# Copying a residual state to HBM in eight queued pieces instead of two

## The chip, the cores and the metric

The kernel runs on one core of one Trainium2 chip. The metric is the device time of one execution in microseconds (us), and the number that is compared is the median of several executions. A profiled execution gives the trace: for each engine every instruction with its start, its duration and what it waited for.

## What is computed

One decoder layer, on x of 256 tokens by 2048 columns, all in float32. The part of the reference that matters here:

```python
h = rms_norm(x, mix_norm_g[i]);  z = h @ w_in[i]          # mixers A (mLSTM) and B (attention) from z
x = x + jnp.concatenate([ha, hb], axis=-1) @ w_out[i]     # 2048 x 2048
h = rms_norm(x, ffn_norm_g[i])
u = h @ w_up[i]                                           # 2048 x 11264
a, g = jnp.split(u, 2, axis=-1);  a = causal_dwconv(a, conv_w[i], conv_b[i])
x = x + (jax.nn.gelu(a, approximate=False) * g) @ w_down[i]
gate = jax.nn.sigmoid(rms_norm(x, ple_norm_g[i]) @ w_ple_gate[i])
x = x + gate * (p[i].astype(x.dtype) @ w_ple_proj[i])
```

The x after w_out is the residual state of this document. It is used twice: at once, normalised, as the left operand of w_up; and much later, when the product with w_down is added to it.

## The kernel before, in words

**Products.** Every float32 operand of a product is held as two parts, a rounded one (`hi`) and the rest (`lo`), and a product is three matmuls (`three`, lines 361 to 364): hi by hi, hi by lo, lo by hi. A weight block arrives by DMA in a raw buffer; `part` (line 294, and line 1291 in the feed-forward stage) casts it to `hi` on ScalarE (line 295 or 1292) and subtracts on VectorE for `lo` (line 297 or 1294). So each block of weights costs a DMA of 512 KB, one cast, one subtraction and 12 matmuls of 512 columns.

**Plain blocks and seven-blocks.** In w_out, w_up and others some pairs of weight rows are multiplied with seven products in place of eight. Such a pair is a group of four blocks, written "a" four times or "b" four times in an order string: the first loads two raw buffers and multiplies one product, each of the others multiplies two. The splits of the third and the fourth add halves of the two raw buffers with VectorE (lines 435, 436, 446 and 447), so the group holds both raw buffers until its fourth split. "p" is a plain block. `OUT_ORDERS` (line 54) holds one order of 20 blocks for each half of the output columns of w_out; the second is that of the output columns 1024 to 2047.

**Streams.** `run_stream` (line 267) writes the program for the blocks up to and with w_out. At block i it splits blocks up to i + 3 and loads as many further blocks as there are free raw buffers: three named `raw` and, in this part, four more (`morex`). Then it writes the block's matmuls, and after them whatever hook was put on the block with `with_after`. `run_units` (line 1300) does the same for the feed-forward blocks, with splits up to four blocks ahead; its raw buffers are the three `raw`, four more (`u32r`, `u36r`) from block 7 on, and `v4`, the half of row tile 0 of `xs` with the columns 1024 to 2047, from block 26 on. The loads, the copies of this change and some layout moves (`move`, line 202, 32 KB each, which go out on SyncE and GpSimd) are DMAs that SyncE issues, one after the other in one queue. A DMA whose operands are not ready holds up all that stand behind it on SyncE.

**The order on an engine is not that of the source.** The program is handed to a scheduler that orders each engine's instructions by an estimate of time, keeping to the dependencies. `tc.issue_after(ins)` adds the one constraint that what the block issues on the engine of `ins` stands behind `ins`. `traced()` returns the last instruction written. `between` (line 1685) puts its hook behind the last cast, the last subtraction and the last load.

**The residual state.** It lives in SBUF in `xs`, 128 partitions by 2 row tiles by 2048 columns. `evac`, `combined` and line 1035 add the w_out products to it. The feed-forward stage needs the space: row tile 1 becomes `z_up` (line 1123, written by lines 1761 to 1764 at the end of the seven-blocks of each w_up group), and row tile 0 becomes `c_` (line 1139) and the raw buffer `v4`. So the state is copied to a DRAM tile `kept_x` (line 79) by `keep_x` and comes back by `move_x` (line 1125) late in the w_down stage. `keep_x(0)`, the columns 0 to 1023, is hooked on block 8 of the second w_out order; `keep_x(1)`, the columns 1024 to 2047, on block 8 of the first w_up group, whose order is "pppppp" "apapapap" "bpbbbp".

Of the kernel before, what the change touches and what calls it, by code (L numbers as in the profile page):

```python
# [50 lines left out]
TURN_AT = (-1, -1, 0, 0)  # L51
GATE_ORDER = "ppppp" "apapapap" "bpbpbb" "p"
OUT_K = (8, 9, 10, 11, 12, 13, 14, 15, 0, 1, 2, 3, 4, 5, 6, 7)
OUT_ORDERS = ("pppp" "apapapap" "bpbpbpb" "p", "pp" "apapapa" "bpbpbb" "ppppp")
ACT_AT = (9, 10, 11, 12, 13, 14, 15, 16, 17, 18)


# [1 line left out]
def layer_kernel(  # L59
# [6 lines left out]
    nc = tc.nc  # L66
# [12 lines left out]
    kept_x = kp.tile([P, NT, D], F32, name="kept_x")  # L79

    def keep_x(i):
        c = slice(i * 1024, (i + 1) * 1024)
        nc.sync.dma_start(out=kept_x[:, :, c], in_=xs[:, :, c])

    def bank(tag, name):
        return ps.tile([P, 512], F32, tag=tag, name=name)
# [1 line left out]
    def f32(ap):  # L88
        return ap.bitcast(F32)
# [8 lines left out]
    xs = bp.tile([P, NT, D], F32, name="xs")  # L98
# [84 lines left out]
    def rstd_of(ssq, name):  # L183
        tot = sm.tile([P, NT], F32, name=f"tot_{name}")
        dve.tensor_reduce(out=tot, in_=ssq, axis=AX.X, op=ALU.add)
        r = sm.tile([P, NT], F32, name=f"rstd_{name}")
        rsqrt_mean(r, tot, D)
        return r
# [40 lines left out]
    last = {}  # L229

    def traced():

        return nc.cur_bb.bb.instructions[-1]
# [7 lines left out]
    def pull(n):  # L241

        while n > 0 and side:
            turn[0] ^= 1
            job = side[min(turn[0], len(side) - 1)]
            try:
                next(job)
                n -= 1
            except StopIteration:
                side.remove(job)  # L250

    def pull_all():
        rush.append(1)
        pull(10 ** 6)
        rush.clear()
# [11 lines left out]
    def run_stream(blocks, pulls, more, ramp=False):  # L267

        nb = len(blocks)
        held, used = set(), {}  # L270
        raw_tags = [f"raw{i}" for i in range(RAW)]

        def free(j):
            tags = [t for t in [*raw_tags, *more] if t not in held and (t in raw_tags or more[t][0] <= j < more[t][1])]
            return sorted(tags, key=lambda t: used.get(t, -1))

        def put(j):
            b = blocks[j]
            if b.load is not None:
                b.load()  # L280
            b.raws, b.tags = [], free(j)[: len(b.srcs)]
            for t, src in zip(b.tags, b.srcs):
                held.add(t)
                kb, n = src.shape[1], src.shape[2]
                raw = wp.tile([P, BLK], F32, tag=t, name=f"raw{j}", bufs=1) if t in raw_tags else more[t][2]()
                nc.sync.dma_start(out=raw[:, : kb * n].rearrange("p (k n) -> p k n", k=kb), in_=src)
                b.raws.append(raw)

        def give(tags):
            for t in tags:  # L290
                held.remove(t)
                used[t] = max(used.values(), default=0) + 1

        def part(hi, lo, raw):
            act.copy(hi, raw)  # L295
            last["hi"] = traced()
            dve.tensor_sub(lo, raw, f32(hi))  # L297

        loaded = split = 0
        for i in range(-RAW, nb):  # L300
            ahead = min(AHEAD_SPLIT, 1 + i // 2) if ramp else AHEAD_SPLIT
            while True:
                if loaded < nb and (i >= -1 or loaded <= i + RAW) and len(free(loaded)) >= len(blocks[loaded].srcs):
                    put(loaded)
                    loaded += 1
                elif i >= -1 and split < min(nb, i + ahead + 1, loaded):
                    j, split = split, split + 1
                    b = blocks[j]
                    if b.prep is not None:
                        b.prep()  # L310
                    hi = wp.tile([P, BLK], F32R, tag=f"hi{j % PARTS}", name=f"hi{j}", bufs=1)
                    lo = wp.tile([P, BLK], F32R, tag=f"lo{j % PARTS}", name=f"lo{j}", bufs=1)
                    if b.own is not None:
                        give(b.own(part, hi, lo))
                        b.parts = hi, lo
                        continue
                    kb, n = b.srcs[0].shape[1:3]
                    hi, lo = hi[:, : kb * n], lo[:, : kb * n]
                    part(hi, lo, b.raws[0][:, : kb * n])
                    give(b.tags)  # L320
                    b.parts = [v.rearrange("p (k n) -> p k n", k=kb) for v in (hi, lo)]
                else:
                    break
            if i >= 0:
                blocks[i].fn(*blocks[i].parts)
                done[0] += 1
                pull(pulls)
# [174 lines left out]
    with mixers:  # L502
# [430 lines left out]
        def with_after(b, hook):  # L933
            fn = b.fn
            b.fn = lambda hi, lo: (fn(hi, lo), hook())
# [86 lines left out]
        def out_group(g_):  # L1022

            st = {}

            def places(h):
                if h == 0:
                    return squares("x2y"), mp.tile([P, NT * 4, 128], F32, tag="col", name="x2z")
                v = [mk_place[:, i * BLK : (i + 1) * BLK] for i in range(2)]
                return v[0].rearrange("p (t b c) -> p t b c", t=NT, b=4), v[1].rearrange("p (a c) -> p a c", c=P)  # L1030

            def evac(t, h, o):
                c = 2 * g_ + h
                xc = xs[:, t, c * 512 : (c + 1) * 512]
                dve.tensor_add(xc, o, xc)
                if g_:
                    return
                if t == 0:
                    st[h] = places(h)
                square(st[h][0], t, 0, xc)  # L1040
                if t == NT - 1:
                    move(*st[h], nc.sync if h else None)
                    side.append(columns((st[h][1], done[0]), get_x2T, c * 4, g_ffn))

            def added():
                for h in range(2):
                    sumsq(ssq2, 2 * g_ + h, 512)

            def combined(p1, p5, p6, p7):
                c0 = g_ * 1024  # L1050
                x00, x01, x10, x11 = (xs[:, t, c0 + n * 512 : c0 + (n + 1) * 512] for t in range(NT) for n in range(2))
                right = xs[:, :, c0 + 512 : c0 + 1024]
                a = mqT.rearrange("p g a c -> p (g a c)")[:, g_ * 512 : (g_ + 1) * 512]
                act.copy(a, p1)
                dve.tensor_add(x00, p1, x00)
                dve.tensor_add(a, p6, a)
                dve.tensor_add(right, p5.unsqueeze(1).broadcast_to([P, 2, 512]), right)
                dve.tensor_sub(x01, x01, a)
                dve.tensor_add(a, p7, a)
                dve.tensor_add(x10, x10, a)  # L1060
                dve.tensor_sub(x11, x11, a)

            n7 = len(set(OUT_ORDERS[g_]) - {"p"})
            ks = OUT_K if n7 == 2 else (*OUT_K[:2], *OUT_K[4:8], *OUT_K[2:4], *OUT_K[8:])
            return pair_group(w_out, lambda: catT, g_ * 1024, 512, OUT_ORDERS[g_], (("mm", "aux"), ("aux", "mm"))[g_],
                              lambda r: S_o["t"][:, r], evac, added, combined, ks, 2 * g_)

        for g_ in range(2):
            grp = out_group(g_)
            if g_ == 0:  # L1070
                fn = grp[4].fn
                grp[4].fn = lambda hi, lo, fn=fn: (pull_all(), fn(hi, lo))
            else:
                with_after(grp[8], lambda: keep_x(0))
            blocks.extend(grp)

        def third(i):
# [10 lines left out]
    with tc.tile_pool(name="ffn", bufs=1) as fp:  # L1088
# [596 lines left out]
        def between(hook):  # L1685
            def f():
                with tc.issue_after(last["hi"]), tc.issue_after(last["lo"]), tc.issue_after(last["load"]):
                    hook()
            return f
# [101 lines left out]
        us = []  # L1791
        for q in range(KF // 4):
            us += up_group(q)
        first_late = len(us)
        with_after(us[8], between(lambda: keep_x(1)))
        with_after(us[3], between(lambda: r2.update(t=rstd_of(ssq2, "ffn"))))
        for r, i in enumerate((2, 9)):
            with_after(us[i], between(lambda r=r: up_sums(r)))
# [61 lines left out]
```

## Time and profile before

| what | value |
|---|---|
| median of 3 runs | 1232.29 us (1231.33 to 1235.31) |
| the profiled execution's own time | 1232.22 us |
| its span, first to last instruction | 1230.4 us |
| granted TensorE clock | 0.999 |
| VectorE busy | 1009.7 us (82%) |
| ScalarE busy | 757.0 us (62%) |
| HBM read, written | 247.99 MB, 8.93 MB |

In the profile PE is TensorE, PEld its weight load, DVE VectorE, ACT ScalarE, POOL GpSimd and SP SyncE; SPq is an instruction by which SP issues a DMA. L83 is line 83 of the kernel. A row of the chain or of the timeline has the start and the duration in us, the engine, the line, the operation and the tiles it writes and reads; a bracket at its end gives how long the engine had been idle and what it waited for. A row of waits has who waited for whom, the total in us, how many times, and the longest. A row of stretches has the busy time of each engine with the number of instructions, the granted clock, the share of time in which the DMA engines were busy, and the rate. A row of DMA issues has the tiles, the size and the us from issue to landing.

### The profile page before, as it was taken

What the parts mean: (1) busy time and instruction counts of PE and PEld (TensorE: products, weight loads), DVE (VectorE), ACT (ScalarE), POOL (GpSimd) and SP (SyncE); (2) the same over time, 40 slices, a digit from 0 to 9 for tenths busy, and PEclk for the clock granted to TensorE, in tenths of its full rate; (3) what the DMA queues carried; (4) which work ended last, traced back from release to release, by engine and by line L of the source; (5) the groups of instructions that cost most, each with busy time, mean ns of one, the idle gap of its engine ahead of it and who ended that gap; (6) DMA issues with size and microseconds to landing.
All of it is one profiled execution on the core that took longest, in us unless ns stands there. A gap on an engine that the chain in (4) does not pass through costs nothing.

```text
span 1230.4 us, 16417 instructions
## 1 busy us (share of the span) xinstructions
PE 1223.2 (99%) x5589; PEld 1030.4 (84%) x5589; DVE 1009.7 (82%) x1262; ACT 757.0 (62%) x1109; POOL 172.9 (14%) x321
## 2 busy tenths in 40 slices
PE   9999999999999999999999999999999999999998
PEld 7999988888888788888888888888888888888887
DVE  6788857675679988788998898998788999999773
ACT  8567545565655665766676676757656656556652
POOL 2011237243301201011101100110110000050000
PEclk9999999999999999999999999999999999999999
DMA  9566587676566677767687678656797896776560
GB/s 305 182 195 196 170 235 223 186 216 188 169 229 214 197 250 244 234 217 236 208 275 241 185 250 272 224 173 221 236 304 245 302 369 207 265 252 213 194 226 35
DMA packets 127718, 276.37 MB, mean 225 GB/s; under 512 B 14682, under 2 KB 25042, under 8 KB 127634
## 3 DMA queue, kind: packets, MB, share of 16 engines
q1 hardware_dynamic: 116560, 257.73, 65.6%
q0 software_dynamic: 10688, 17.43, 5.0%
q8 instruction: 44, 0.72, 0.2%
q14 instruction: 41, 0.33, 0.1%
q10 hardware_dynamic: 385, 0.16, 0.1%
HBM read 247.99 MB, written 8.93 MB: 209 GB/s over the span
## 4 chain that ended last, share of the span: by engine, by line
PE 96%; DMA 1%; DVE 1%; issue 0%; ACT 0%; SPq 0%; ACTq 0%; DVEq 0%
PE up L364 12%; PE up L362 12%; PE up L363 11%; PE tg L351 6%; PE tg L352 6%; PE tg L353 6%; PE pg L362 4%; PE pg L363 4%; PE pg L364 4%; PE dnP L1342 1%; PE dnP L1344 1%; PE dnP L1343 1%; PE upP L363 1%; PE upP L364 1%; PE upP L362 1%; PE gt L363 1%
## 5 line engine op out<-in xcount | busy, mean ns | idle before, releaser
L363 PE MATMUL up<-part,x2T 128*128 128x512 f32 x608 | 237.0, 390 | 0.0
L364 PE MATMUL up<-part,x2T 128*128 128x512 f32 x608 | 236.6, 390 | 0.0
L1292 ACT CAST part<-raw 128x1024 fp32r<-128x1024 f32 (+1 forms) x144 | 145.9, 1022 | 109.3 <-PE up L364 34.9
L297 DVE TENSOR_TENSOR lo<-raw,hi 128x1024 fp32r<-128x1024 f32 (+3 forms) x119 | 139.2, 1172 | 78.2 <-ACT hi L295 78.0
L362 PE MATMUL up<-part,x2T 128*128 128x512 f32 x608 | 185.6, 390 | 0.0
L1294 DVE TENSOR_TENSOR part<-raw,part 128x1024 fp32r<-128x1024 f32 (+1 forms) x140 | 164.4, 1182 | 20.6 <-ACT part L1292 17.1
L295 ACT CAST hi<-raw 128x1024 fp32r<-128x1024 f32 (+3 forms) x119 | 120.0, 1010 | 99.5 <-PE tg L353 44.9
L363 PEld LDWEIGHTS up<-part,x2T 128*128 128x128 f32 x608 | 114.2, 188 | 23.6
L364 PEld LDWEIGHTS up<-part,x2T 128*128 128x128 f32 x608 | 114.2, 188 | 23.5
L362 PEld LDWEIGHTS up<-part,x2T 128*128 128x128 f32 x608 | 114.2, 188 | 23.6
L353 PE MATMUL tg<-hi,hT 128*128 128x512 f32 x288 | 113.7, 396 | 0.0
L352 PE MATMUL tg<-lo,hT 128*128 128x512 f32 x288 | 113.4, 394 | 0.0
L351 PE MATMUL tg<-hi,hT 128*128 128x512 f32 x288 | 112.5, 397 | 0.0
L206 POOL DMA_DIRECT2D EZ<-Y x66 | 35.0, 538 | 359.0 <-issue 166.6
L1292 ACT CAST part<-u36r 128x1024 fp32r<-128x1024 f32 (+1 forms) x46 | 47.8, 1042 | 35.4 <-PE up L364 17.7
L1294 DVE TENSOR_TENSOR part<-u36r,part 128x1024 fp32r<-128x1024 f32 (+1 forms) x46 | 55.6, 1209 | 10.0 <-ACT part L1292 5.8
L352 PEld LDWEIGHTS tg<-lo,hT 128*128 128x128 f32 x288 | 54.2, 188 | 10.9
L353 PEld LDWEIGHTS tg<-hi,hT 128*128 128x128 f32 x288 | 54.2, 188 | 10.9
L351 PEld LDWEIGHTS tg<-hi,hT 128*128 128x128 f32 x288 | 53.9, 188 | 10.6
L1294 DVE TENSOR_TENSOR part<-u32r,part 128x1024 fp32r<-128x1024 f32 (+1 forms) x44 | 50.4, 1148 | 12.1 <-ACT part L1292 10.5
L1292 ACT CAST part<-u32r 128x1024 fp32r<-128x1024 f32 (+1 forms) x44 | 43.4, 991 | 22.2 <-PE up L364 9.0
L363 PE MATMUL pg<-lo,hT 128*128 128x430 f32 (+1 forms) x156 | 55.8, 358 | 0.0
(936 smaller groups left out, 2765.6 us busy)
## 6 DMA issues: line engine op xcount, KB each, us to landing
raw<-in_w_up_dram SPq DMA_DIRECT2D x78, 512.0 KB, 5.1
raw<-in_w_in_dram SPq DMA_DIRECT2D x71, 512.0 KB, 4.4
u36r<-in_w_up_dram SPq DMA_DIRECT2D x43, 512.0 KB, 5.8
raw<-in_w_down_dram SPq DMA_DIRECT2D x41, 512.0 KB, 5.6
u32r<-in_w_up_dram SPq DMA_DIRECT2D x34, 512.0 KB, 4.8
xs<-in_w_up_dram SPq DMA_DIRECT2D x21, 512.0 KB, 5.1
w2b<-in_w_down_dram SPq DMA_DIRECT2D x20, 512.0 KB, 5.8
raw<-in_w_out_dram SPq DMA_DIRECT2D x17, 512.0 KB, 5.2
```

Source lines behind the costliest of these rows:

```text
L206: (other if other and (4 * a + b) % 3 else pool).dma_start(out=c[32 * b : 32 * b + 32, a::4], in_=y[32 * a : 32 * a + 32, :, b])
L295: act.copy(hi, raw)
L297: dve.tensor_sub(lo, raw, f32(hi))
L351: pe.matmul(o, ah, hi[:, i, :], start=first, stop=False)
L352: pe.matmul(o, ah, lo[:, i, :], start=False, stop=False)
L353: pe.matmul(o, al, hi[:, i, :], start=False, stop=last)
L362: pe.matmul(o, ah, hi, start=start, stop=False)
L363: pe.matmul(o, ah, lo, start=False, stop=False)
L364: pe.matmul(o, al, hi, start=False, stop=stop)
L1292: act.copy(r32(hi), raw)
L1294: dve.tensor_sub(r32(lo), raw, hi)
L1342: pe.matmul(o, ah, hi, start=first, stop=False)
```

## The change

`keep_x(i)` copies 256 columns in place of 1024, so that there are eight calls in place of two. Each is written inside `tc.issue_after(last["load"])`, and `run_stream` now records its last load as `run_units` did already. Pieces 0 to 3 hang on the blocks 3, 6, 9 and 12 of the second w_out order, pieces 4 to 7 on the blocks 6, 8, 10 and 12 of the first w_up group. In the second w_out order one plain block moves from the end to the place between the last "a" and the first "b".

```diff
-OUT_ORDERS = ("pppp" "apapapap" "bpbpbpb" "p", "pp" "apapapa" "bpbpbb" "ppppp")
+OUT_ORDERS = ("pppp" "apapapap" "bpbpbpb" "p", "pp" "apapapap" "bpbpbb" "pppp")
...
     def keep_x(i):
-        c = slice(i * 1024, (i + 1) * 1024)
-        nc.sync.dma_start(out=kept_x[:, :, c], in_=xs[:, :, c])
+        c = slice(i * 256, (i + 1) * 256)
+        with tc.issue_after(last["load"]):
+            nc.sync.dma_start(out=kept_x[:, :, c], in_=xs[:, :, c])
...
                 nc.sync.dma_start(out=raw[:, : kb * n].rearrange("p (k n) -> p k n", k=kb), in_=src)
+                last["load"] = traced()
                 b.raws.append(raw)
...
-                with_after(grp[8], lambda: keep_x(0))
+                for i in range(4):
+                    with_after(grp[3 + 3 * i], lambda i=i: keep_x(i))
...
-        with_after(us[8], between(lambda: keep_x(1)))
+        for i in range(4):
+            with_after(us[6 + 2 * i], between(lambda i=i: keep_x(4 + i)))
```

## The prediction

> **What bounds the kernel now.** I read the page first, then who waited for whom on PE, then the busy time by stretches.
>
> ```profile
> span 1230.4 us, 16417 instructions
> PE 1223.2 (99%) x5589; PEld 1030.4 (84%) x5589; DVE 1009.7 (82%) x1262; ACT 757.0 (62%) x1109; POOL 172.9 (14%) x321
> ```
> ```profile
> PE warm L106 <- DVE ones L102: 1.1, 1, 1.1
> PE pg L362 <- ACT hi L295: 0.9, 1, 0.9
> PE xT L168 <- DMA xs<-in_x_dram: 0.8, 1, 0.8
> ```
> ```profile
> 0.00:50.00 50.00, 48.12 (x236) 42.33 (x237) 34.22 (x56) 36.38 (x80) 7.62 (x24) 1.00 0.79 257
> 400.00:450.00 50.00, 49.10 (x224) 40.22 (x223) 43.95 (x62) 32.10 (x48) 7.54 (x14) 1.00 0.67 214
> 450.00:500.00 50.00, 50.00 (x222) 41.44 (x221) 42.13 (x46) 30.04 (x38) 3.20 (x6) 1.00 0.81 261
> 1200.00:1231.00 31.00, 26.02 (x160) 23.23 (x158) 10.89 (x17) 6.73 (x10) 0.00 (x0) 0.96 0.10 34
> ```
>
> PE is idle for 1230.4 - 1223.2 = 7.2 us in all: 1.9 us in the first 50 us, 0.9 us between 400 and 450, and 30.4 - 26.0 = 4.4 us behind the last products. The change touches 392 to 465 us. There PE loses 0.9 us, once. Adding no matmul and removing none, the change can hardly gain more than this one wait; everything else that it can do is to make new ones. The wait is in the w_out stage, where PE stands for a cast:
>
> ```profile
> 414.02 0.39 PE L363 MATMUL pg<-lo,catT 128*128 128x512 f32 x1
> 414.25 0.39 PE L364 MATMUL pg<-hi,catT 128*128 128x512 f32 x1
> 415.53 0.96 PE L362 MATMUL pg<-hi,catT 128*128 128x512 f32 x3 [0.90 <-ACT hi L295]
> ```
> ```profile
> 409.51 1.05 ACT L295 CAST hi<-morex 128x1024 fp32r<-128x1024 f32 x1
> 413.49 1.05 ACT L295 CAST hi<-raw 128x1024 fp32r<-128x1024 f32 x1 [2.92 <-DMA raw<-in_w_out_dram]
> 414.44 1.04 ACT L295 CAST hi<-morex 128x1024 fp32r<-128x1024 f32 x1
> ```
>
> Matmuls start 0.23 us apart (414.02 to 414.25); here the step is 1.28 us, so 1.05 us is lost. PE goes on when the cast that began at 414.44 is through. That cast, of a morex buffer, stood on ACT behind the cast of a raw buffer, which had waited 2.92 us for its DMA. The issues of SP, and the landings of the load and of the copy:
>
> ```profile
> 392.39 0.62 SPq L83 DMA_DIRECT2D kept_x<-xs  x1
> 395.25 0.33 SPq L286 DMA_DIRECT2D raw<-in_w_out_dram  x1
> 395.88 6.50 SPq L206 DMA_DIRECT2D mkT<-mkT  x10
> 402.47 0.53 SPq L286 DMA_DIRECT2D raw<-in_w_out_dram  x1
> 403.04 0.92 SPq L286 DMA_DIRECT2D morex<-in_w_out_dram  x2
> 404.24 4.94 SPq L286 DMA_DIRECT2D raw<-in_w_out_dram  x2
> 410.89 0.64 SPq L1269 DMA_DIRECT2D raw<-in_w_up_dram  x1
> ```
> ```profile
> raw<-in_w_out_dram SPq DMA_DIRECT2D x1, 512.0 KB, 9.1
> kept_x<-xs SPq DMA_DIRECT2D x1, 1024.0 KB, 4.6
> ```
>
> The load issued at 404.24 took 9.1 us and landed at 413.3; the cast began at 413.49. This chain (landing, cast, cast, PE) has no slack: a microsecond more on that landing is a microsecond more of time, and 1.05 us less removes the wait. The copy at 392.39 had landed by 397.0, so it no longer stood in this load's way.
>
> **The change part by part.** First, where the w_out pieces go. At block i the stream has split up to i + 3 and holds seven raw buffers. In the new order the seven blocks of "a" are 2, 4, 6, 8 and those of "b" 10, 12, 14, 15. At block 3 the seven buffers hold the pair of 2, then 7, 9, the pair of 10, and 11: piece 0 stands behind the load of block 11, the group's eleventh load, which in the trace is the one at 395.25 (the group has 16 loads, and five in these rows follow it). At block 6 they hold the pair of 10, 11, 13, 16, 17, 18: piece 1 stands behind the load of 18, one of the burst from 403.04 to 404.24. At blocks 9 and 12 all loads are written, so pieces 2 and 3 stand behind the load of 19, the second one of the row at 404.24.
>
> Taken away is the transfer of 1 MB from 392.4 to 397.0. It delays nothing on PE today and its end is 5 us ahead of the burst: 0 us. Piece 0 adds one issue of about 0.62 us (the row of 392.39) at 395.6, before the ten moves at 395.88; these start 0.3 us later, and so do the loads at 402.47 to 403.6. The late load itself waits for something else:
>
> ```profile
> 399.20 0.69 DVE L297 TENSOR_TENSOR lo<-morex,hi 128x512 fp32r<-128x512 f32 x1
> 399.93 0.69 DVE L435 TENSOR_TENSOR morex<-morex 128x512 f32<-128x512 f32 x1
> 402.39 0.69 DVE L436 TENSOR_TENSOR morex<-morex,morex 128x512 f32<-128x512 f32 x1
> 403.00 1.22 DVE L297 TENSOR_TENSOR lo<-raw,hi 128x1024 fp32r<-128x1024 f32 x1
> ```
>
> The buffer comes free at 403.00 + 1.22 = 404.22, when the fourth split of "a" has been subtracted, and the load goes out at 404.24. Three instructions of "b" (0.69 us each, 2.07 us) stand in front of that subtraction on DVE. With a plain block put between "a" and "b", these three belong to later blocks; the plain block's own subtraction (1.22 us, as the row of 403.00) may come in their place. That is 2.07 - 1.22 = 0.85 us less, at most 2.07 us less, at worst nothing, if the scheduler keeps other work there. I take 0.85 us earlier for the buffer; the SP queue, 0.3 us later than now, then lets the load out near 404.
>
> The larger part of the wait is an order: on ACT the raw buffer's cast stands ahead of the morex buffer's, though that one's load was issued first. One load of 512 KB takes these rates:
>
> ```profile
> 406.00:408.00 2.00, 2.00 (x11) 1.65 (x10) 2.00 (x3) 1.06 (x1) 1.00 (x2) 1.00 0.89 218
> 408.00:410.00 2.00, 2.00 (x11) 1.65 (x10) 1.79 (x3) 1.45 (x2) 0.00 (x0) 1.00 1.01 380
> ```
>
> 512 KB at 218 to 380 GB/s is 1.4 to 2.4 us, so the morex data was there by about 411 to 412, and cast in its turn it would be through by 413.1, before PE wanted it at 414.5. Either repair, the earlier landing by about 1 us or the other order, ends the wait: -1.05 us. Both follow from the order of the blocks, not from the pieces.
>
> Piece 1 is the danger. It is written behind the load of block 18. If SP issues that load ahead of the late one (a morex load did go ahead of it), the piece comes between: its issue costs 0.62 us and its 256 KB cost 0.7 us at 380 GB/s or 1.2 us at 218 GB/s. That is 1.3 to 1.8 us on the chain without slack. If the late load goes first, piece 1 costs it nothing. Freed at 403.4 instead of 404.22 it is written and ready before the load of 18, so I take nothing, and keep 1.8 us for the range. Pieces 2 and 3 stand behind the last load of the stage; they put 1.24 us of issue into the gap before 410.89 and 1.4 to 2.4 us of traffic ahead of the first w_up loads, whose casts come later: 0 us, the cover being PE's work on the last four w_out blocks, 48 matmuls at 0.23 us or 11 us.
>
> Then the feed-forward pieces. By the same count with splits up to i + 4, piece 4 stands behind the load of block 15, piece 5 behind that of 19, pieces 6 and 7 behind that of 22. In the trace:
>
> ```profile
> 452.65 0.54 SPq L1269 DMA_DIRECT2D u36r<-in_w_up_dram  x1
> 453.23 0.61 SPq L83 DMA_DIRECT2D kept_x<-xs  x1
> 453.94 0.56 SPq L1269 DMA_DIRECT2D raw<-in_w_up_dram  x1
> 456.67 0.54 SPq L1269 DMA_DIRECT2D u36r<-in_w_up_dram  x1
> 462.31 0.54 SPq L1269 DMA_DIRECT2D xs<-in_w_up_dram  x1
> ```
> ```profile
> SPq L1269 <- DMA kept_x<-xs: 5.0, 1, 5.0
> ```
> ```profile
> kept_x<-xs SPq DMA_DIRECT2D x1, 1024.0 KB, 9.0
> ```
> ```profile
> 479.90 1.05 ACT L1292 CAST part<-raw 128x1024 fp32r<-128x1024 f32 x1 [5.20 <-PE up L364]
> ```
>
> The load into xs (`v4`) waits for the copy's landing: 453.23 + 9.0 = 462.2. SP stands for 5.0 us, and PE does not feel it: its row of 450 to 500 is full, and ACT has 5.20 us to spare before the cast at 479.90. Pieces 6 and 7 go out at 457.2 and 457.9 (behind 456.67 + 0.54). A 256 KB piece is not in this trace; between a move of 32 KB, median 3.9 us (the last row of this part), and the 9.0 us I take 4.5 us, nearest to the small end because no load is issued beside it. SP is then freed at 462.4, as now; at 9.0 us it would be 466.9, 4.6 us later, inside the 5.20 us. So 0 us. The first write over these columns of row tile 1 is later than that:
>
> ```profile
> 473.34 1.23 DVE L1764 TENSOR_TENSOR xs<-upP,xs 128x1024 f32<-128x1024 f32 x1
> ```
> ```profile
> DMA to landing us min/median/max: 2.5/3.9/6.2
> ```
>
> The sum against the profiled execution: span 1230.4 - 1.05 = 1229.35, and with the 1.8 us outside the span (1232.22 - 1230.4) 1231.2 us. That execution stands 0.07 us under the median of the runs, so the median is forecast at 1231.2 us too, a change of 0.1%. About 0.3%, 3.7 us, is what a measurement of this kernel can tell from no change: the line lies at 1228.6 and 1236.0.
>
> **The rivals.**
>
> *The wait stays as it is.* The raw buffer comes free when DVE is done, DVE is without a gap there (2.00 of 2.00 us in the row of 406), and the scheduler may keep the order of the two casts. Then nothing changes: 1232.3 us. For it speaks that block 17 is in the same place of both orders and is wanted at the same time.
>
> *Piece 1 in front of the late load.* The place is SP at 404, the price 1.3 to 1.8 us, and it decides if the load of block 18 is issued ahead of the one that waits for DVE. Then the wait grows to 2.4 to 2.9 us: 1233.6 to 1234.1 us, say 1233.9, slower than before. For it speaks that the raw load was the last of the four at 402.47 to 404.24; against it, that DVE gets lighter.
>
> *A piece costs a landing, not its bytes.* A move of 32 KB takes 3.9 us to land and a copy of 1 MB 4.6 us; nearly all is fixed. If the queue spent that fixed time on each piece in turn, the late load would come 0.62 + 3.9 = 4.5 us later: 1236.8 us. Against it: SP issues ten moves in 6.50 us, 0.65 us apart, so transfers overlap. The Trainium skill, "DMA: Bandwidth & Descriptors", section Bandwidth, has a rule against this change: "Batch DMAs to ≥1 MiB for ≥75% of peak"; its section Anatomy of one DMA gives 2.0 us plus the bytes over 436 GB/s, measured on the GpSimd path. By that formula, as an estimate, a copy of 1 MB takes 4.4 us, where the trace has 4.6, and a piece 2.6 us; spent in turn, this would make 1232.3 + 0.62 + 2.6 = 1235.5 us.
>
> *The scheduler moves something else.* The copy at 392.39 went out ahead of six loads, five of which the source puts before it, so small edits can reorder an engine. This has no place that I can name and either sign; the later stages run with PE full.
>
> **How the numbers follow.** The wait goes: 0.40, at 1231.2. It stays: 0.29, at 1232.3. Piece 1 in front: 0.18, at 1233.9. A piece costs a landing: 0.05, at 1236.8. Reordered elsewhere: 0.08, of which half is slower by more than 3.7 us and a quarter faster. The range takes in the first three cases, with 1 us below the first and 1.5 us above the 1234.1 of the third, half of the 3.0 us by which the slowest run of before stands over its median: 1230.2 to 1235.6. It leaves out the landing case and most of the last one. Slower by over 0.3%: 0.05 + 0.04 = 0.09. Faster by over 0.3%: 0.02, since PE has no 3.7 us of idle time in the stages that change. Within: 0.89.
>
> **What would show it.** Right: PE's wait for `hi` L295 is gone from its rows, four copies stand on SP between 395 and 411 and four between 449 and 459, each lands in 3 to 6 us, SP still stands about 5 us for kept_x, and the stretch 400 to 450 is full. The piece in front of the late load would show as L83 between two L286 near 404, and a wait of 2 to 3 us on PE; the landing case as loads that land 3 us or more later than now behind a piece. The prediction is wrong if PE waits in a stretch after 450, or if the time leaves 1230.2 to 1235.6.

## The result and the profile after

The changed kernel is slower: median 1237.80 us of 6 runs (1236.93 to 1240.00) against 1231.94 us (1231.33 to 1235.31) for the kernel before on the same chip. The ratio is 1.0045, with a 95% interval of 1.003 to 1.006. The prediction was 1231.2 us in a range of 1230.2 to 1235.6, so the time left the range. The ratios in this document compare undisturbed executions; one of `e1_order` (1356.10 us) and one of `e7_after_chain` (4504.52 us) ran disturbed and are left out of the ratios, though not out of the medians. The profiled execution after took 1236.93 us with a span of 1235.2 us, 4.8 us longer than before.

The page of the kernel after, then its busy time by stretches (us; PE, PEld, DVE, ACT, POOL, each with its number of instructions; granted clock; DMA share; GB/s):

```profile
span 1235.2 us, 16423 instructions
PE 1225.8 (99%) x5589; PEld 1030.5 (83%) x5589; DVE 1010.0 (82%) x1262; ACT 756.8 (61%) x1109; POOL 176.7 (14%) x321
```
```profile
400.00:450.00 50.00, 47.95 (x217) 38.70 (x217) 41.80 (x60) 30.84 (x47) 9.40 (x14) 1.00 0.72 231
450.00:500.00 50.00, 48.40 (x205) 39.16 (x204) 42.09 (x47) 26.04 (x31) 3.19 (x6) 0.97 0.73 227
```

The work is the same: 5589 matmuls. Before, these two stretches held 224 and 222 of them; now they hold 217 and 205. That is 24 fewer, and at 0.227 us apart 5.4 us of PE time, a little more than the 4.8 us by which the span grew: the whole difference arose between 400 and 500 us. The second stretch, full before, is no longer full, and its granted clock is 0.97. Who waited for whom on PE in the kernel after, its start-up waits left out:

```profile
PE upP L364 <- DVE x2T L161: 1.1, 1, 1.1
PE pg L364 <- ACT hi L297: 1.0, 1, 1.0
PE upP L365 <- DVE part L1297: 0.8, 1, 0.8
PE upP L366 <- DVE S_up L473: 0.7, 1, 0.7
```

The wait for `hi` that was to go is still there (1.0 us, 0.9 before). Three new ones stand behind it, all in the first w_up group, for work of DVE. They lie close together in PE's timeline:

```profile
449.63 0.50 PE L364 MATMUL upP<-part,x2T 128*128 128x512 f32 x1 [1.08 <-DVE x2T L161]
...
452.00 0.49 PE L365 MATMUL upP<-part,S_up 128*128 128x512 f32 x1 [0.78 <-DVE part L1297]
453.20 0.79 PE L366 MATMUL upP<-part,S_up 128*128 128x512 f32 x1 [0.71 <-DVE S_up L473]
453.79 1.91 PE L366 MATMUL up<-part,x2T 128*128 128x512 f32 x4
455.50 0.63 PE L364 MATMUL up<-part,x2T 128*128 128x512 f32 x1
455.93 0.63 PE L365 MATMUL up<-part,x2T 128*128 128x512 f32 x1
```

Behind the last wait the matmuls start 0.43 us apart (455.50 to 455.93) where they normally start 0.227 us apart. Stretches cut at these places, after first, then the same 9 us of the kernel before:

```profile
448.00:457.00 9.00, 6.33 (x20) 4.19 (x19) 5.92 (x12) 3.34 (x5) 1.75 (x1) 0.81 0.51 147
449.00:453.70 4.70, 2.47 (x6) 1.25 (x7) 4.55 (x9) 1.67 (x3) 0.75 (x1) 0.94 0.68 178
453.70:456.50 2.80, 2.80 (x8) 2.22 (x8) 0.23 (x1) 0.72 (x1) 0.00 (x0) 0.50 0.51 176
```
```profile
448.00:457.00 9.00, 9.00 (x43) 7.50 (x41) 8.41 (x13) 5.47 (x7) 0.00 (x0) 1.00 0.65 176
```

Twenty matmuls in place of 43 between 448 and 457: 23 x 0.227 = 5.2 us, nearly all of the loss. 2.6 us of it are the three waits (1.08 + 0.78 + 0.71). About 1.4 us are seven matmuls at half pace (7 x 0.2), in a stretch whose granted clock is 0.50. The rest lies in the restarts around the waits, for which the trace names no releaser. A PE that is "busy" for all of 2.80 us did 8 matmuls in it: the busy share alone would not have shown this part.

Now back to where it begins. First ACT in the kernel after, then DVE, then DVE of the kernel before:

```profile
413.64 2.94 ACT L297 CAST hi<-morex 128x1024 fp32r<-128x1024 f32 x3 [5.00 <-DMA morex<-in_w_out_dram]
416.49 1.04 ACT L297 CAST hi<-raw 128x1024 fp32r<-128x1024 f32 x1
```
```profile
414.72 3.50 DVE L299 TENSOR_TENSOR lo<-morex,hi 128x1024 fp32r<-128x1024 f32 x3 [2.22 <-ACT hi L297]
418.13 1.22 DVE L299 TENSOR_TENSOR lo<-raw,hi 128x1024 fp32r<-128x1024 f32 x1
...
425.37 1.22 DVE L1297 TENSOR_TENSOR part<-raw,part 128x1024 fp32r<-128x1024 f32 x1
...
436.80 1.23 DVE L1297 TENSOR_TENSOR part<-raw,part 128x1024 fp32r<-128x1024 f32 x1 [3.21 <-ACT part L1295]
```
```profile
414.57 1.22 DVE L297 TENSOR_TENSOR lo<-raw,hi 128x1024 fp32r<-128x1024 f32 x1 [1.43 <-ACT hi L295]
...
421.90 1.22 DVE L1294 TENSOR_TENSOR part<-raw,part 128x1024 fp32r<-128x1024 f32 x1
```

Before, ACT cast the raw buffer at 413.49 and DVE subtracted it at 414.57. Now ACT stands for 5.00 us, until a morex load has landed; three morex casts then come in one row, the raw one is fourth, and its subtraction starts at 418.13, 3.6 us later than before. The first subtraction of the w_up stage moves from 421.90 to 425.37. DVE then runs dry at 433.6 with four w_up blocks done, where before it had five done by 433.7, and stands for 3.21 us (2.77 us before). The fifth subtraction starts at 436.80, before at 432.49.

Which blocks these casts belong to is read from the numbers of their buffers in the program; the views leave these numbers out. Blocks are counted from 0 within the second w_out group; x2T is the operand that ACT prepares in between:

```
ACT's order of the casts
before   13 12 15 14 17 16 x2T 18 19      (last b-block: 14)
after    14 12 13 18 16 15 17 x2T 19      (last b-block: 15)
```

Block 18 has moved to the front of 16, 15 and 17. Its load is the last morex load of the stage. SP in the kernel after:

```profile
403.39 0.43 SPq L287 DMA_DIRECT2D morex<-in_w_out_dram  x1
403.92 0.38 SPq L287 DMA_DIRECT2D raw<-in_w_out_dram  x1
404.35 0.56 SPq L287 DMA_DIRECT2D morex<-in_w_out_dram  x1
404.95 0.58 SPq L84 DMA_DIRECT2D kept_x<-xs  x1
405.62 0.66 SPq L287 DMA_DIRECT2D raw<-in_w_out_dram  x1
406.33 1.38 SPq L84 DMA_DIRECT2D kept_x<-xs  x2
410.12 17.04 SPq L1272 DMA_DIRECT2D raw<-in_w_up_dram  x4
...
429.24 0.54 SPq L1272 DMA_DIRECT2D raw<-in_w_up_dram  x1
```

The raw load of block 17 goes out at 403.92, a little earlier than the 404.24 of before. It no longer sets the wait: the casts of 16, 15 and 17 queue on ACT behind that of 18, whose load went out at 404.35 and let the cast begin at 413.64. PE, which needs 16 first, goes on at 415.69, when the second cast of that row is through. In the w_up stage the fifth raw load goes out at 429.24, where before it went at 410.89 + 16.11 - 0.54 = 426.46.

Why 18 can go first: block j keeps its parts in buffer pair j mod 4 (`PARTS`), so 18 takes the pair of 14. In the old order 14 was the last b-block, whose cast and products come late, and 18 had to wait for it. In the new order 14 is the third b-block, done early, and nothing keeps the scheduler from placing 18 ahead of 16, 15 and 17.

### The profile page after: what moved, and what is told of

It is laid out like the page before. It is cut to its first block, busy times and chain, and to the rows that moved or that the text cites. A ratio compares the mean times of both kernels' runs of the same rounds, so it can differ in the third digit from the quotient of the medians.

```text
span 1235.2 us, 16423 instructions
## 1 busy us (share of the span) xinstructions
PE 1225.8 (99%) x5589; PEld 1030.5 (83%) x5589; DVE 1010.0 (82%) x1262; ACT 756.8 (61%) x1109; POOL 176.7 (14%) x321
## 4 chain that ended last, share of the span: by engine, by line
PE 99%; DVE 0%; DMA 0%; issue 0%; SPq 0%; ACT 0%; DVEq 0%; ACTq 0%
PE up L366 12%; PE up L365 11%; PE up L364 11%; PE tg L354 6%; PE tg L353 6%; PE tg L355 6%; PE pg L364 5%; PE pg L365 5%; PE pg L366 5%; PE dnP L1346 1%; PE dnP L1345 1%; PE dnP L1347 1%; PE upP L366 1%; PE upP L364 1%; PE upP L365 1%; PE gt L365 1%
## 5 line engine op out<-in xcount | busy, mean ns | idle before, releaser
L366 PEld LDWEIGHTS up<-part,x2T 128*128 128x128 f32 x608 | 114.7, 189 | 23.7
```

What stands on the lines that cost most here:

```text
L366: pe.matmul(o, al, hi, start=False, stop=stop)
```

## The experiments

The theory (C, and O for the block order as a whole): the new block order lets block 18's cast go first, and what follows makes DVE late in the w_up stage. The rivals: the pieces' traffic (D, T), the feed-forward pieces (F), an order of PE in which products on `S_up` stand too early (P, against L: DVE is late and PE waits anyway), and the buffer of one w_up load. In the expectations "unit" and "u" with a number are blocks too.

### The block order alone, and the pieces alone

`e1_order` is the kernel before with the new second string of `OUT_ORDERS` and nothing else. `e2_pieces` is the reverse: the kernel after with the old string.

> The kernel before with the new block order of w_out alone; the copies stay two of 1024 columns. On ACT the cast of block 18, the last but one to be loaded, stands ahead of those of blocks 15, 16 and 17, as in the changed kernel. Theory O (the block order gives a bad order of casts, which frees a raw buffer late and starts the w_up loads late): near 1237.8 us, with waits of PE near 448 us. Theory D (the traffic of the pieces delays the loads): 1231 to 1233 us, no wait near 448.

> All eight pieces with the old block order. Theory O (the loss is the block order's): as the w_out pieces alone, 1230.5 us, no wait of PE at 414 or at 448 us, faster than before by 0.1%. If the pieces did harm of their own in the feed-forward stage: 1232 us or more.

Measured: the order alone 1234.04 us, ratio 1.0018 (1.0005 to 1.0032); the pieces alone 1230.70 us, ratio 0.9992 (0.9983 to 1.0001). PE's waits, the order alone first, then the pieces alone:

```profile
PE upP L362 <- DVE x2T L160: 1.5, 1, 1.5
...
PE pg L362 <- ACT hi L295: 0.7, 1, 0.7
```
```profile
PE pg L364 <- ACT hi L297: 0.4, 1, 0.4
```

And ACT with the order alone:

```profile
413.70 2.94 ACT L295 CAST hi<-morex 128x1024 fp32r<-128x1024 f32 x3 [4.68 <-DMA morex<-in_w_out_dram]
```

The row of three morex casts behind a long wait, and the late x2T on DVE, are there without a single piece. With the pieces and the old order neither is there. All kernels here with the old string and no other constraint on the casts have 17, 16, 18 in that order on ACT, as before; the kernels with the new string that leave casts and buffers alone have 18 ahead of 16, 15 and 17. So the block order is to blame for the sign. It isn't all: order (+2.3 us) and pieces (-1.0 us) together give +5.9, so the pieces make the bad order worse: more than half of the loss is there only with both.

### Half of the pieces

```diff
-                with_after(grp[8], lambda: keep_x(0))
+                for i in range(4):
+                    with_after(grp[3 + 3 * i], lambda i=i: keep_x(i))
...
-        with_after(us[8], between(lambda: keep_x(1)))
+        for i in range(4):
+            with_after(us[6 + 2 * i], between(lambda i=i: keep_x(4 + i)))
```

`e3_wout_pieces` has the first half of this diff alone (pieces 0 to 3, the columns from 1024 on in one copy), `e4_ffn_pieces` the second half alone, both with the old order; `e6_order_wout` is the kernel after with the second half whole, as before.

> The old block order and the old copy in the feed-forward stage; the copy of the columns 0 to 1023 in four pieces behind loads. The casts stand in the order of the kernel before, and piece 1 goes out ahead of the load of block 18. Theory D: 1236 to 1238 us. Theory O: 1232 to 1234 us, the wait near 414 us at most 1.8 us longer by the piece in front of a load.

> The old block order and the old copy in the w_out stage; the copy of the columns 1024 to 2047 in four pieces behind loads. Theories O and D: 1232 us, no wait of PE after 450 us. A theory F, that the feed-forward pieces hold up SP and with it the loads: over 1235 us, with a wait behind 462 us.

> The changed kernel with the old copy of 1024 columns in the feed-forward stage. Theory O: as the block order alone, near 1237 to 1238 us. Theory D: also near 1237 to 1238 us, but then the block order alone is fast. Theory F: 1232 us.

Measured: pieces 0 to 3 alone 1230.45 us, ratio 0.9986 (0.9976 to 0.9996), the only part of the change that clearly gains. Pieces 4 to 7 alone 1232.01 us, ratio 1.0004 (0.9993 to 1.0015). The kernel after without pieces 4 to 7 1237.63 us, ratio 1.0043 (1.0028 to 1.0058), with the same waits as the kernel after. The feed-forward pieces cost nothing, with either order: F falls, and so does D for the pieces by themselves. What pieces 0 to 3 change ahead of PE's wait is seen on SP and ACT of `e2_pieces`, which has them too:

```profile
403.90 0.33 SPq L287 DMA_DIRECT2D raw<-in_w_out_dram  x1
404.28 0.57 SPq L84 DMA_DIRECT2D kept_x<-xs  x1
404.89 0.76 SPq L287 DMA_DIRECT2D morex<-in_w_out_dram  x1
```
```profile
412.65 1.05 ACT L297 CAST hi<-raw 128x1024 fp32r<-128x1024 f32 x1 [2.42 <-DMA raw<-in_w_out_dram]
413.60 1.04 ACT L297 CAST hi<-morex 128x1024 fp32r<-128x1024 f32 x1
```

Before, both morex loads went out ahead of this raw load (404.24, cast at 413.49). Now the raw load stands ahead of the second of them, with piece 1 between, and its cast starts at 412.65: 0.84 us earlier, and PE's wait falls from 0.9 to 0.4 us, half of the 1.0 us by which the median is lower. With pieces 0 to 3 alone it is gone.

### The casts in the order of the blocks

```diff
         def part(hi, lo, raw):
-            act.copy(hi, raw)
+            with tc.issue_after(last["hi"]) if chained[0] else nullcontext():
+                act.copy(hi, raw)
```

`chained` is on for the 20 blocks of the second group. `e7_after_chain` is the kernel after with this, `e10_pieces_chain` is `e2_pieces` with it.

> The changed kernel with one constraint: the casts of the 20 blocks of the second w_out order stand on ACT in the order of the blocks. Theory C (the cast of block 18 ahead of those of 15, 16 and 17 starts the whole loss): the wait at 414 is gone, the second w_up load goes out by 417 instead of 419.4 us, the waits at 448 are gone, 1230 to 1232 us. Theory T (the traffic of three pieces among the last w_out loads is enough): 1235 us or more.

> All eight pieces, the old block order, and the casts of the second w_out order in the order of the blocks. If the order of casts is still worth something where the late load has been repaired: under 1230 us; else 1230.5 us as the pieces alone.

Measured: after with the chain 1235.07 us, ratio 1.0017 (1.0006 to 1.0028); the executions behind that ratio lie between 1231.79 and 1236.20 us, the profiled one at 1233.51. The pieces with the chain 1231.85 us, ratio 0.9998 (0.9989 to 1.0007), 1.1 us above the pieces alone, with a new wait of PE of 0.9 us for `lo` at 416. The time of the first is not the 1230 to 1232 us that C expected; its median lies where T begins, at 1235, so this time does not decide between them. In its profile all the waits of PE at 415 and at 449 to 454 are gone, and another stands at 441. PE's wait, the stretch behind it, and ACT:

```profile
PE up L367 <- ACT x2T L160: 2.8, 1, 2.8
```
```profile
441.50:446.00 4.50, 4.50 (x22) 3.47 (x21) 4.50 (x10) 3.57 (x6) 1.08 (x1) 1.00 0.82 289
```
```profile
440.11 0.62 ACT L1298 CAST part<-raw 128x512 fp32r<-128x512 f32 x1 [1.09 <-DMA raw<-in_w_up_dram]
440.64 1.56 ACT L160 ACTIVATE x2T<-xT,vT 128x256 fp32r<-128x256 f32 x4
```

ACT's four x2T stand behind a w_up cast that waits for its DMA. So the waits of the kernel after go with the order of the casts, but the chain moved other things too and pays for them. It left open whether the order of casts is all of it.

### PE's order

`e11_after_pe_order` is the kernel after with the third a-block's products of the first w_up group, those on `S_up`, put behind the second's.

```diff
+                    last["fn2"] = traced()
...
-                    sum_of(5, S(1), half(hi, 0), half(lo, 0))
+                    with tc.issue_after(last["fn2"]) if q == 0 else nullcontext():
+                        sum_of(5, S(1), half(hi, 0), half(lo, 0))
```

> The changed kernel with one constraint on PE: in the first w_up group the six products of the third a-block stand behind those of the second. SP keeps its order, ACT and DVE all but a few instructions. Theory P (three products with the sums S_up, put on PE ahead of seven others that are ready, cost the time from 450 to 456 us, the slow matmuls included): 1234 us, as the block order alone, and the wait for x2T at 448 stays, 1 to 1.5 us. Theory L (DVE is late by its late loads and PE would wait for it anyway): 1236 to 1238 us.

Measured: 1239.10 us, ratio 1.0059 (1.0046 to 1.0071), slower still. PE waits 1.1 us at 449.85 as before, and then for the last x2T; behind that it runs at half clock:

```profile
PE up L366 <- DVE x2T L161: 3.0, 1, 3.0
```
```profile
453.80:459.50 5.70, 5.70 (x13) 4.46 (x14) 1.57 (x2) 2.03 (x2) 0.00 (x0) 0.50 0.27 89
```

With the `S_up` products out of the way PE stands until 453.80: the products that now come first wait for an x2T of DVE themselves. P falls: in either order DVE is late and PE waits for it.

### The buffer of one w_up load

In the kernel after, w_up's block 0 is loaded second and its load waits until 419.38 for the subtraction of block 17. `run_units` takes the three `raw` buffers in the order of their names; here it takes them in the order in which `run_stream` gave them back:

```diff
+                freed[t] = len(freed_order)
+                freed_order.append(t)
...
+        for t in (f"raw{i}" for i in range(RAW)):
+            used[t] = freed[t] - len(freed_order)
```

The instruction order of every engine stays as it was, but for the two loads, which exchange their buffers and their places. `e12_after_first_free` is the kernel after with it, `e13_pieces_first_free` the pieces with the old block order, `e14_before_first_free` the kernel before.

> The kernel after, but the first three loads of the w_up stream take the three raw buffers in the order in which the last loads of w_out free them; every engine issues the same instructions in the same order as in the kernel after, only the buffers of the first loads change places. Theory L (the loss after 448 us comes from w_up's block 0, whose load is second in the queue and waits until 419.4 us for the split of w_out's block u17): block 0's load is issued at about 410 us, its cast begins near 420 instead of 423.9, the waits of PE on x2T (1.1), part (0.8) and S_up (0.7) between 449 and 454 us shrink to under 0.5 us in sum, the half-pace products at 455 go with them, and the time falls from 1237.7 to 1232 to 1234 us; the 1.0 us wait at 414 us stays. Rival A (the late casts of w_out themselves delay the x2T and S_up work on DVE and ACT, whichever buffer the load takes): the waits at 449 to 454 stay within 0.5 us of 2.6 in sum and the time is 1236.5 to 1238.

> All eight pieces with the old block order, and the buffers of w_up's first loads in the order in which w_out frees them; every engine's order is as with the eight pieces alone. There PE has no wait between 440 and 460 us, so theory L gives nothing to win: 1230.2 to 1231.2 us, ratio 0.998 to 1.000. Rival A gives the same. If it comes below 1230.0, the second load's lateness had cost something with the old block order too, which neither theory holds.

> The kernel before with w_up's first buffers in the order in which w_out frees them; all engines' orders as before. No wait of PE after 440 us is there to be removed, and the wait of 0.9 us at 415 us is ahead of the w_up loads: 1231 to 1232.5 us, ratio 0.999 to 1.001 by theory L and by rival A. It is the measure for the same edit in the kernel after: what that gains beyond this one is the late load's price.

Measured: 1238.34 us, ratio 1.0052 (1.004 to 1.0065); 1230.01 us, ratio 0.9988 (0.9979 to 0.9997); 1231.34 us, ratio 0.9999 (0.999 to 1.0007). PE's waits and SP in the first:

```profile
PE upP L367 <- DVE x2T L161: 1.1, 1, 1.1
...
PE upP L368 <- DVE part L1302: 0.8, 1, 0.8
PE upP L369 <- DVE S_up L476: 0.7, 1, 0.7
```
```profile
409.82 17.00 SPq L1277 DMA_DIRECT2D raw<-in_w_up_dram  x4
...
428.90 0.54 SPq L1277 DMA_DIRECT2D raw<-in_w_up_dram  x1
```

The first w_up cast on ACT no longer waits for its load (0.78 us in the kernel after) and starts at 422.63, where it was 423.87. PE's waits did not change. This refutes what I held then, that one late load of w_up is the link. DVE works through its queue in order and had its subtractions for w_out and x2T in front; the fifth load went out at 428.90, as late as ever. The rival held: whichever buffer that load takes, the late casts of w_out delay the rest.

### One dependency put back

`e16_after_swap_parts` keeps the new block order and all pieces. Only the last two b-blocks, 14 and 15, exchange their pairs of `hi` and `lo` buffers, so that 18 again shares a pair with the last b-block:

```diff
+                    s = {nb - 6: nb - 5, nb - 5: nb - 6}.get(j, j)
-                    hi = wp.tile([P, BLK], F32R, tag=f"hi{j % PARTS}", name=f"hi{j}", bufs=1)
-                    lo = wp.tile([P, BLK], F32R, tag=f"lo{j % PARTS}", name=f"lo{j}", bufs=1)
+                    hi = wp.tile([P, BLK], F32R, tag=f"hi{s % PARTS}", name=f"hi{j}", bufs=1)
+                    lo = wp.tile([P, BLK], F32R, tag=f"lo{s % PARTS}", name=f"lo{j}", bufs=1)
```

> The kernel after, but the last two b-blocks of w_out, units 14 and 15, exchange their pairs of hi and lo buffers, so that unit 18's cast has to wait for the last b-block, 15, as it did in the block order before. The pieces, the block order and the loads of w_out stay as in the kernel after; ACT's order becomes 14, 16, 15, 17, 19, 18 and the fifth w_up load goes ahead of the two u32r loads. Theory C (what the new block order costs is that it sets unit 18's cast free to go first): the waits of PE on x2T (1.1), part (0.8) and S_up (0.7) at 449 to 454 us and the half-pace products behind them go, and the time falls from 1237.8 to 1231 to 1234 us, ratio 0.999 to 1.002; the wait on hi near 414 us may stay, at up to 1.1 us. Rival (the block order itself is bad, by whatever casts: the three products on S_o that now stand elsewhere, or DVE's own order): PE still loses over 2 us at 448 to 456 and the time is 1236 to 1239 us.

Measured: 1230.77 us, ratio 0.9993 (0.9984 to 1.0002). From 1237.8 to 1230.8 us by two exchanged buffers. ACT's order is now 14, 16, 15, 17, 19, x2T, 18; its casts of 16 and 15, and the stretch that lost 5.2 us. The start of this execution is slower: PE waits 1.9 us for its first rows of x, where the kernel after waits 0.6, and runs some ten matmuls at half pace behind them (218 matmuls in the first 50 us in place of 237), so the w_out stage stands 3.8 us later in it:

```profile
414.86 1.06 ACT L297 CAST hi<-morex 128x1024 fp32r<-128x1024 f32 x1 [0.71 <-PE pg L367]
416.15 1.05 ACT L297 CAST hi<-morex 128x1024 fp32r<-128x1024 f32 x1 [0.23 <-DVE morex L450]
```
```profile
452.00:461.00 9.00, 9.00 (x42) 7.43 (x41) 8.66 (x13) 4.22 (x4) 0.00 (x0) 1.00 0.73 227
```

The 5.00 us for which ACT stood have become 0.71 and 0.23. All of PE's waits between 400 and 500 us are gone, the one at 415 too, and so is the half clock. Theory C is shown as the cause: with block 18 tied down again, the new order and the pieces cost nothing and are level with the pieces alone. T falls with it: all the pieces are still there.

What stays open is each link between the late casts and the wait at 449. It isn't the second w_up load (`e12`). The lateness of the fifth goes with the loss. Executions start differently, so it is counted here from the w_out load that SP issues right behind the ten moves. It goes out 24.0 us after that in the kernel before and 23.7 to 24.6 us after it in `e2`, `e3`, `e4`, `e10`, `e13`, `e14` and `e16`, none of which waits at 449; 25.1 us after it in `e1_order`, with one wait of 1.5 us; and 26.3 to 26.4 us after it in the kernel after, `e6`, `e11` and `e12`, which lose most. This is also where the order alone and the order with the pieces part. No run moves this load alone, so it may be a link or only another effect. Freeing block 18 changes the scheduler's orders on ACT, DVE and PE together, and the exchange of buffers also frees block 19, which now shares a pair with 14; I did not separate these further.

No version stands clearly above the others that gain: `e3_wout_pieces` (0.9986) and `e13_pieces_first_free` (0.9988) beat the kernel before by about 0.1%, both with the old block order.

## Why the prediction was wrong, point by point

**The failing step** is "Either repair, the earlier landing by about 1 us or the other order, ends the wait: -1.05 us. Both follow from the order of the blocks, not from the pieces." The wait did not end, and the second sentence is wrong too. The raw load did go out earlier, at 403.92 ("near 404"), and the order of the casts did change. But I considered only an exchange of two casts, the raw one and the morex one ahead of which it stood. The new order freed a third, of block 18, which had not been able to go early, and it took the front and held up the others for 5.00 us. What shortens the wait is the pieces: 0.9 to 0.4 us with all of them, to nothing with the first four, while the order alone leaves 0.7 us. The second repair as such was sound: in `e16_after_swap_parts`, with 18 tied down, ACT casts 16 ahead of 17, at 414.86 or 411.1 on the time scale of the kernel after, and PE has no wait there.

**The ground for "the later stages run with PE full"** was the second failure. It made the rival "the scheduler moves something else" a case of 0.08 without a place. The place was 449 to 454 us. In the kernel before, this stretch of DVE was there to be read:

```profile
440.00:450.00 10.00, 10.00 (x49) 8.27 (x48) 9.99 (x19) 5.61 (x9) 0.71 (x1) 1.00 0.41 114
```

DVE is busy for 9.99 of 10.00 us just ahead of the products that need it. PE was full, but on a DVE without slack in these 10 us. DVE had idle time shortly before: between 425 and 440 us it was busy for 11.23 of 15.00 us. The kernel after could not use that time (10.61 of 15.00 us there), because ACT waited for the fifth w_up load; so the fifth subtraction, from 432.49 before, moved to 436.80, toward the full stretch. These rows fit the loss, but no run shows this link by itself.

**Piece 1** was put in the right place, and the 0 us taken for it was right. It went out at 404.95, behind the load of 18 and behind that of 17, and did not delay the raw load; the rival that had it in front of the late load did not come about. **Pieces 2 and 3** went out behind the last load of the stage, as said, at 406.33 and 407.0; 0 us was right by `e2_pieces` and `e3_wout_pieces`.

**A piece costs a landing:** refuted. In the window from 395 to 432 us of the kernel after, the row of the four pieces of w_out (the last number is the median us to landing):

```profile
kept_x<-xs SPq DMA_DIRECT2D x4, 256.0 KB, 9.6
```

That is near the 9.1 us that the raw load took before: three of them go out within 2.8 us and land with the loads around them, side by side; the pieces alone give 1230.7 us, not 1236.8. I had expected 3 to 6 us. The Trainium skill, "DMA: Bandwidth & Descriptors", section Bandwidth, asks for transfers of 1 MiB and more; the formula of the same page's section Anatomy of one DMA, spent in turn, gave 1235.5 us. The 1230.7 us of the pieces alone decide against spending it in turn.

**The feed-forward pieces** at 0 us: right. Only the size of their delay was off. The last one went out at 466.06 in the kernel after, not 457.9, and the load into `xs` at 471.71 where 462.31 was before; PE did not wait for it, and `e4_ffn_pieces` is level with the kernel before.

**Two small readings** were off without consequence. The 3.9 us to landing are those of the x2z moves, which GpSimd issues; the ten moves on SP between 390 and 412 us have a median of 3.3 us. And the first write over the columns 1024 to 2047 of row tile 1 is that of line 1763 at 472.6, not that of line 1764 at 473.34.

**The sum** was thus off by one term: -1.05 us was forecast for the order; with the pieces in place it costs about 7 us (1237.8 - 1230.7 = 7.1). The pieces, forecast at 0, gain 1.0 us in the medians (1231.66 to 1230.70), an effect whose interval just reaches no change.

## What to carry to other kernels

Where blocks rotate through a few buffers, moving one block in a list changes which blocks share a buffer, and with that which orders a scheduler may choose: look for the step that the move sets free, not only for those that it reorders. A stretch in which PE is full has slack only if the engine that feeds it has idle time that it can use there; read that engine's busy time before calling the stretch safe. A change made of several edits is worth running edit by edit: here the edit in the title was level by itself or gained 0.1%, and the move of one block in a list beside it turned that into a loss of 0.45%.

## What the runs showed of the hardware

I had not expected PE to lose clock from waits as short as these. After three waits of 1.08, 0.78 and 0.71 us within 5 us, in which PE was busy for 2.47 of 4.70 us, the granted clock was 0.50 for 2.8 us and seven matmuls started 0.427 us apart. With 1.08 and 2.99 us of waiting (`e11_after_pe_order`) it was 0.50 for 5.7 us and 13 matmuls. A single wait of 2.83 us (`e7_after_chain`) between full stretches left the clock at 1.00, and so did one of 1.46 us (`e1_order`). At the start of `e16_after_swap_parts`, waits of 1.1 and 1.9 us were followed by ten matmuls 0.427 us apart, but the profile gives a granted clock of 1.00 for them; the two records disagree there, and I draw nothing from it. The Trainium skill, "TensorE: Matmul & The Clock Gate", section "HAM oscillation — how this bites in real kernels", puts the rule as no idle gaps of PE over about 3.4 us. Here no wait was that long, the longest 2.99 us, and the clock still halved, so the measurement decides against it as a safe bound: in these two kernels two or three shorter waits within 5 us were enough. That the half-rate start-to-start time for 512 columns is 426.7 ns, as the same page says in its section "Wait — 56ns, not 53.3ns?", agrees with the 0.427 us of the trace.
